# ReGLU MLP: w1 block 0's value half loaded behind four x blocks, the fifth x block turned as 32 bit, two casts moved to VectorE, gate products of three x blocks by one

## The chip, the cores and the metric

The kernel runs on one core of a Trainium2 chip. The metric is the device time in microseconds (us). Before the change it was 309.19 us (median of three runs, 309.01 to 309.37).

Engines are named as in the profile: PE (TensorE matmul), PEld (its weight loads), DVE (VectorE), ACT (ScalarE), POOL (GpSimd), SP (SyncE, which issues the transfers here).

## The reference

```python
# x: 16 x 256 x 512, w1: 512 x 4096, w2: 2048 x 512, all float32
h = x @ w1
gate, value = np.split(h, 2, axis=-1)
h = np.maximum(gate, 0) * value
return (h @ w2).astype(np.float32)
```

## The kernel before

The kernel works on 16 bit operands and saves products by a scheme in which seven products of halves replace eight (P1 to P7 of a block). The scheme needs sums of quarters of x (S1 to S4) and differences of quarters of w1 (T1 to T4). At the start these do not exist yet. So the first two blocks of 128 hidden columns (blocks 0 and 1) are computed plainly, from x as it arrives; from block 2 on the scheme takes over.

The change touches only this opening, about the first 20 us. There x comes as eight blocks of 128 rows by 512 columns, 256 KB each. I count them one to eight: one to four are the first half, `xn[0]` in the code, and five to eight the second. They are transposed on PE ("turned") and copied out of PSUM to 16 bit. A w1 block comes as a gate half and a value half; each is 256 KB for blocks 0 and 1, and 512 KB for the pair 2/3.

```python
fetch_first(0, (0, 1))                       # x blocks one, two
first_w = [load_w1(nc.sync, *wl[0])]         # w1 block 0: gate half, value half
fetch_first(0, (2, 3))
first_w.append(load_w1(nc.sync, *wl[1]))     # w1 block 1: gate half, value half
...
fetch_first(1, range(4))                     # x blocks five to eight
fetch(2, nc.sync); fetch(3, nc.sync)         # w1 blocks 2/3, then 4/5 (one line each in the kernel)
...
plain_w(0, 0, (pool, dve))                   # casts of block 0's gate half
arm(YS[0]); arm(YS[1])
plain[0].open()
plain[0].part("gate", *first_half, cols(0, 2))
plain_w(0, 1, (pool, dve))
keep_busy(4)                                 # filler: products nobody reads
plain[0].part("value", *first_half, cols(0, 2))
turn_first(xo, 0, 2, ...); keep_busy(1); turn_first(xo, 0, 3, ...)
...
plain[1].part("gate", *first_half)           # "block 1's gate": the first use of w1 block 1
cast_first(0, dve); cast_first(1, pool); cast_first(2, pool); cast_first(3, pool)
...
```

At the end of the opening three things come together on DVE and POOL:

```python
for n in ("S1", "S2", "S3"):
    sum_of(sums[1], n)                       # DVE: last sums of x
sum_of(xo, "S4")                             # DVE: two 128 x 1024 inputs in SBUF
held()                                       # DVE: block 1's gate product; frees a PSUM bank
prepare(2, False)
sum_w1(6)                                    # POOL: T1, T2, ... of w1 blocks 2/3
```

Of the kernel before, what the change touches and what calls it, by code (L numbers as in the profile page):

```python
# [16 lines left out]
P = 128  # L17
# [9 lines left out]
@with_exitstack  # L27
def kernel(ctx: ExitStack, tc: tile.TileContext, x, w1, w2, out):






    nc = tc.nc
    x2 = x.flatten_outer_dims()
    out2 = out.flatten_outer_dims()
    flagpool = ctx.enter_context(tc.tile_pool(name="flagpool", bufs=1))
    flag = flagpool.tile([1, 1], dt.int32, name="flag")
    with ExitStack() as fast:  # L40
        unfit = fast_way(fast, tc, x2, w1, w2, out2, flag)
    with tc.If(unfit > 0, label="general"):
        with ExitStack() as general:
            general_way(general, tc, x2, w1, w2, out2)
# [52 lines left out]
def fast_way(ctx, tc, x2, w1, w2, out2, flag):  # L97
# [9 lines left out]
    nc = tc.nc  # L107
# [37 lines left out]
    ident = wpool.tile([P, P], F32, name="ident")  # L145
# [5 lines left out]
    def keep_busy(n):  # L151

        for _ in range(n):
            nc.tensor.matmul(Y[:, :TH // 2], warm_b[:, :P], warm_b[:, :TH // 2], start=False, stop=True,  # L154
                             skip_group_check=True)


    def x_tiles():

        o = {n: xpool.tile([P, 2, TH], F16, name=f"x_{n}", tag=f"x_{n}")  # L160
             for n in ("A11", "A12", "A22", "S1", "S2", "S3", "S4")}
        o["A21"] = o["S3"]
        return o
# [50 lines left out]
    def load_w1(eng, jb, n, u, vs=(0, 1)):  # L214
        t = w_stage[:, u:u + n].rearrange("p u v -> p (u v)").rearrange("p (g e j) -> p g e j", g=2, e=4)
        for v in vs:
            eng.dma_start(out=t[:, v], in_=w1_v[v, :, :, jb * P:(jb + n) * P])
        return t.rearrange("p g (k b) j -> p k b g j", k=2)
# [215 lines left out]
    wl = [(0, 1, 0), (1, 1, 1)] + [(jb, 2, jb % 6) for jb in range(2, NJ, 2)]  # L434
    ws, copies = {}, []

    def fetch(i, eng):
        if i < len(wl):
            assert all(j > i - 3 for j, _ in copies)
            jb, n, u = wl[i]  # L440
            ws[i] = load_w1(eng, jb, n, u)
# [3 lines left out]
    def sum_w1(n=None):  # L445
        for job in w_sums[:n]:
            job()
        del w_sums[:n]

    def prepare(i, at_once=True):  # L450
        jb, n, _ = wl[i]
        copies.extend((i, c) for c in w1_ops(jb, n, ws.pop(i), 1 if i == 2 else n))
        if at_once:
            sum_w1()

    def copy_some(n):
        for _, c in copies[:n]:
            c()
        del copies[:n]

    def plain_w(i, v, engines):

        (jb, n, _), t = wl[i], first_w[i]
        js = slice(jb * P, (jb + n) * P)
        for k, (n, copy) in enumerate(zip((("B11", "B21"), ("T3", "B22"))[v], engines)):
            copy(out=wop[n][:, :, js], in_=t[:, k, :, v])  # L466
# [13 lines left out]
    xn = [[t.rearrange("p a b -> p (a b)").bitcast(F32) for t in place[4 * h:4 * h + 4]] for h in range(2)]  # L480

    x16_first = [halfs.tile([P, 8, P], F16, name="xh", tag="xh").rearrange("p (b q) c -> p b (q c)", b=2) for _ in range(2)]
    ident16 = wpool.tile([P, P], F16, name="ident16")
    half, other = (0, TH // 2), (TH // 2, TH)

    def fetch_first(h, bs):
        for b in bs:
            nc.sync.dma_start(out=xn[h][b], in_=x_nat[0, h, b])  # L488

    def cast_first(b, copy):  # L490
        copy(out=x16_first[b // 2][:, b % 2], in_=xn[1][b])

    def turn_first(o, h, b, places, copies):

        rows, one = (x16_first[b // 2][:, b % 2], ident16) if h else (xn[0][b], ident)
        for k in range(2):
            for e in range(2):
                nc.tensor.transpose(places[k][:, e * P:(e + 1) * P],  # L498
                                    rows[:, (2 * k + e) * P:(2 * k + e + 1) * P], one)
        for k in range(2):  # L500
            copies[k](out=o[f"A{h + 1}{k + 1}"][:, :, b * P:(b + 1) * P],
                      in_=places[k].rearrange("p (b t) -> p b t", b=2))

    def new_x():
        return psx.tile([P, TH], F32, name="X", tag="X")
# [4 lines left out]
    def new_y():  # L510
        return psy.tile([P, TH], F32, name="Y", tag="Y")

    def arm(ps):

        nc.tensor.matmul(ps, warm_b[:, :P], warm_b[:, :TH], start=True, stop=True)

    dve, act, pool = nc.vector.tensor_copy, nc.scalar.copy, nc.gpsimd.tensor_copy
    fetch_first(0, (0, 1))
    first_w = [load_w1(nc.sync, *wl[0])]
    fetch_first(0, (2, 3))  # L520
    first_w.append(load_w1(nc.sync, *wl[1]))
    make_identity(nc, ident)
    fetch_first(1, range(4))
# [3 lines left out]
    xo = x_tiles()  # L527
    plain = [Plain(g, jb) for jb in range(NPLAIN)]
    first_half, second_half = (xo["A11"], xo["A12"]), (xo["A21"], xo["A22"])
    YS = [new_y(), new_y()]  # L530

    def halves(*ts, c=0):
        return [t[:, c:c + 2 * P] for t in ts]

    def turns(t):
        return [t.bitcast(F16)[:, c:c + 2 * P] for c in (0, 2 * P)]

    def cols(b, n=1):
        return b * P, (b + n) * P

    turn_first(xo, 0, 0, halves(*YS), (dve, act))
    XS = [new_x(), new_x()]
    turn_first(xo, 0, 1, halves(*XS), (dve, act))
    plain_w(0, 0, (pool, dve))
    arm(YS[0])
    arm(YS[1])
    plain[0].open()
    plain[0].part("gate", *first_half, cols(0, 2))
    plain_w(0, 1, (pool, dve))
    keep_busy(4)  # L550
    plain[0].part("value", *first_half, cols(0, 2))
    turn_first(xo, 0, 2, halves(*XS, c=2 * P), (dve, act))
    keep_busy(1)
    turn_first(xo, 0, 3, halves(*YS, c=2 * P), (dve, act))
    plain_w(1, 0, (pool, dve))
    plain_w(1, 1, (pool, dve))
    for b in (2, 3):
        for which in ("gate", "value"):
            plain[0].part(which, *first_half, cols(b), False)
    fetch(4, nc.sync)  # L560
    plain[0].value()
    plain[1].open()
    plain[1].part("gate", *first_half)
    cast_first(0, dve)
    cast_first(1, pool)
    cast_first(2, pool)
    cast_first(3, pool)
    plain[1].part("value", *first_half, half)
    turn_first(xo, 1, 0, (turns(YS[0])[0], turns(YS[1])[0]), (dve, act))
    plain[0].gate(0)  # L570
    plain[1].part("value", *first_half, other, False)
    spare = plain[0].X, plain[1].W
    plain[1].value()
# [3 lines left out]
        plain[0].part(which, *second_half, cols(0))  # L577
    turn_first(xo, 1, 1, (turns(YS[0])[1], turns(YS[1])[1]), (dve, act))
    turn_first(xo, 1, 2, (turns(spare[0])[0], turns(spare[1])[0]), (dve, act))
    xo["S3"] = tmp.tile([P, 1024], F16, name="sq", tag="sq", bufs=1).rearrange("p (a b) -> p a b", a=2)  # L580
    sums = [{n: t[:, :, slice(*c)] for n, t in xo.items()} for c in (half, other)]
    sum_of(sums[0], "S1")
# [4 lines left out]
        sum_of(sums[0], n)  # L587
    for which in ("gate", "value"):
        plain[0].part(which, *second_half, cols(2), False)
    for which in ("gate", "value"):  # L590
        plain[0].part(which, *second_half, cols(3), False)
    plain[1].open(*reversed(YS))
    plain[1].part("gate", *second_half)
    for n in ("S1", "S2", "S3"):
        sum_of(sums[1], n)
    sum_of(xo, "S4")
    held()
    prepare(2, False)
    sum_w1(6)
    copy_some(1)  # L600
    plain[0].value()
    plain[0].gate(1)
    copy_some(1)
    prepare(3, False)
    w_sums[:4] = [w_sums[i] for i in (2, 0, 3, 1)]
    sum_w1()
# [49 lines left out]
    rows = []  # L656
# [9 lines left out]
    for s in range(NS):  # L666
# [74 lines left out]
        if s + 1 < NS:  # L741
            xo = xo_next
# [47 lines left out]
```

## Time and profile before

| | before |
|---|---|
| time, median of 3 | 309.19 us |
| PE busy, of the span | 300.7 of 307.5 us |
| 16 DMA engines | full from about 5 to 20 us (0.7 busy from 4 to 5) |
| block 1's gate starts | 10.37 us |
| P1 / P5 / P6 of block 2 start | 16.21 / 17.94 / 18.56 us |
| last product of the kernel starts | 302.66 us |

The profile page's first part gives the busy time of each engine and its share of the span, and its fourth part the chain of waits that ended last.

```profile
PE 300.7 (98%) x1905; PEld 184.0 (60%) x1905; DVE 235.9 (77%) x388; ACT 176.4 (57%) x348; POOL 151.4 (49%) x189
...
PE 96%; DMA 1%; SPq 0%; POOL 0%; ACT 0%; issue 0%
```

PE is the whole chain. So only what makes PE wait in the opening can be worth anything. This is the timeline of PE in the kernel before. Its columns are start, duration, engine, line of the program, operation with output and inputs, shape and count, and in brackets how long the engine had been idle and what ended that.

```profile
6.96 0.61 PE L325 MATMUL X<-x_A,w_B 128*128 128x256 f16 x4 [0.98 <-POOL w_B L466]
7.40 0.60 PE L154 MATMUL Y<-warm 128*128 128x256 f16 x4
...
8.71 0.27 PE L154 MATMUL Y<-warm 128*128 128x256 f16 x1
...
10.37 1.04 PE L325 MATMUL X<-x_A,w_B 128*128 128x512 f16 x4
...
14.17 0.28 PE L498 MATMUL X<-ident,xh 128*128 128x128 f16 x2
...
16.21 0.59 PE L250 MATMUL X<-x_A,w_B 128*128 128x512 f16 x2
...
17.94 0.59 PE L250 MATMUL W<-x_S,w_T 128*128 128x512 f16 x2
18.56 0.60 PE L250 MATMUL Y<-x_S,w_T 128*128 128x512 f16 x2
19.00 0.59 PE L250 MATMUL X<-x_A,w_B 128*128 128x512 f16 x2
...
20.30 0.59 PE L250 MATMUL Y<-sq,w_T 128*128 128x512 f16 x2
```

6.96 is the first gate product; 7.40 and 8.71 are the filler, five products in all. 10.37 is block 1's gate, 14.17 the turn of x block eight, and 16.21, 17.94 and 18.56 are P1, P5 and P6 of block 2. Two products of 128x512 take 0.43 us. So the step from 17.94 to 18.56 (0.62) holds a wait of 0.19, though no bracket shows it: a small gap hides in the modelled ends of the products. Starts are the thing to read here. The 19.00 is P1 of block 3, and 20.30 is P7 of block 2.

Next, the timelines of DVE and of POOL where the two meet, in the kernel before.

```profile
16.15 0.42 DVE L169 TENSOR_TENSOR sq<-x_A,x_S 128x512 f16<-128x512 f16 x1
16.49 0.68 DVE L169 TENSOR_TENSOR x_S<-x_A,x_S 128x1024 f16<-128x1024 f16 x1
17.09 1.28 DVE L334 SCALAR_TENSOR_TENSOR g<-X,v 128x512 f16<-128x512 f32 x2
```

```profile
16.48 1.27 POOL L232 TENSOR_TENSOR w_T<-w_stage 128x256 f16<-128x256 f32 x1 [2.49 <-DMA w_stage<-in_w_dram]
17.83 0.67 POOL L232 TENSOR_TENSOR w_T<-w_stage,w_T 128x256 f16<-128x256 f32 x1
18.46 1.41 POOL L232 TENSOR_TENSOR w_T<-w_stage 128x256 f16<-128x256 f32 x2
```

POOL's first difference (T1) starts 0.14 after its data has landed (16.34) and takes 1.27 us. The same work later takes 0.70 each (the line with x2). It stands behind DVE's sum S4, which started at the same moment. T2 ends at 18.50, and P6, which needs it, starts at 18.56.

**Landings.** Each transfer signals 16 times in the trace; I call the last of the 16 its landing. In this trace: x blocks one and two 3.62 and 4.25, w1 block 0 gate and value 6.32 and 7.11, x three and four 8.13 and 8.82, w1 block 1 gate and value 9.73 and 10.61, x five to eight 11.29, 11.97, 12.65 and 13.33, w1 blocks 2/3 gate and value 14.83 and 16.34. In the timelines a landing shows as the start of the cast that waited for it, 0.02 to 0.06 later.

### The profile page before, as it was taken

What the parts mean: (1) busy time and instruction counts of PE and PEld (TensorE: products, weight loads), DVE (VectorE), ACT (ScalarE), POOL (GpSimd) and SP (SyncE); (2) the same over time, 40 slices, a digit from 0 to 9 for tenths busy, and PEclk for the clock granted to TensorE, in tenths of its full rate; (3) what the DMA queues carried; (4) which work ended last, traced back from release to release, by engine and by line L of the source; (5) the groups of instructions that cost most, each with busy time, mean ns of one, the idle gap of its engine ahead of it and who ended that gap; (6) DMA issues with size and microseconds to landing.
All of it is one profiled execution on the core that took longest, in us unless ns stands there. A gap on an engine that the chain in (4) does not pass through costs nothing.

```text
span 307.5 us, 5285 instructions
## 1 busy us (share of the span) xinstructions
PE 300.7 (98%) x1905; PEld 184.0 (60%) x1905; DVE 235.9 (77%) x388; ACT 176.4 (57%) x348; POOL 151.4 (49%) x189
## 2 busy tenths in 40 slices
PE   7999999999999999999999999999999999999994
PEld 6844444588844444478864444458884444448883
DVE  2579888899768888887438888889536888888841
ACT  2488886455865555538845555546865555553231
POOL 2389999800069899200029889700007998700000
PEclk9999999999999999999999999999999999999998
DMA  6976779964765260001354910000335110001132
GB/s 207 357 257 190 227 177 174 225 123 87 270 193 86 69 136 3 0 0 67 136 175 103 207 34 2 0 2 24 115 108 167 35 34 0 3 1 34 53 120 74
DMA packets 35837, 32.88 MB, mean 107 GB/s; under 512 B 14432, under 2 KB 31328, under 8 KB 35680
## 3 DMA queue, kind: packets, MB, share of 16 engines
q1 hardware_dynamic: 33536, 26.22, 28.0%
q0 software_dynamic: 2272, 6.29, 11.4%
q8 instruction: 16, 0.26, 0.4%
q14 instruction: 13, 0.11, 0.1%
HBM read 27.26 MB, written 12.58 MB: 130 GB/s over the span
## 4 chain that ended last, share of the span: by engine, by line
PE 96%; DMA 1%; SPq 0%; POOL 0%; ACT 0%; issue 0%
PE Y L250 26%; PE X L250 17%; PE W L250 17%; PE Y L362 14%; PE X L362 9%; PE W L362 9%; DMA w_stage<-in_w_dram 1%; PE X L325 1%; PE W L325 1%; PE Y L325 1%; PE Y L498 0%; PE X L498 0%; SPq L488 0%; PE Y L154 0%; POOL w_B L466 0%; ACT o L405 0%
## 5 line engine op out<-in xcount | busy, mean ns | idle before, releaser
L250 PEld LDWEIGHTS <-w_T 128*128 128x128 f16 x496 | 48.3, 98 | 57.3 <-POOL w_T L232 1.1
L179 POOL TENSOR_TENSOR fold<-xh 128x1024 f32<-128x1024 f16 x16 | 30.3, 1894 | 94.5 <-DMA xh<-x 93.7
L250 PE MATMUL X<-x_A,w_B 128*128 128x512 f16 x248 | 73.8, 379 | 0.0
L250 PE MATMUL Y<-x_S,w_T 128*128 128x512 f16 x220 | 65.5, 379 | 0.0
L250 PEld LDWEIGHTS <-w_B 128*128 128x128 f16 x372 | 36.4, 98 | 42.0
L277 DVE SCALAR_TENSOR_TENSOR cc<-W,pu 128x512 f32<-128x512 f32 x62 | 42.9, 691 | 21.2 <-ACT pu L271 20.4
L257 ACT COPY Y<-X 128x512 f32<-128x512 f32 x62 | 35.4, 571 | 38.2 <-PE X L250 37.9
L271 ACT ACTIVATE pu<-Y 128x512 f32<-128x512 f32 x62 | 37.1, 598 | 33.9 <-PE Y L250 32.9
L182 POOL TENSOR_TENSOR fold<-fold 128x512 f32<-128x512 f32 (+2 forms) x96 | 51.8, 539 | 7.5
L362 PEld LDWEIGHTS <-w_stage 128*128 128x128 f16 x512 | 50.0, 98 | 5.8
L287 DVE SCALAR_TENSOR_TENSOR cc<-Y,pu 128x512 f32<-128x512 f32 x62 | 42.9, 691 | 6.7
L282 DVE SCALAR_TENSOR_TENSOR g<-X,cc 128x512 f16<-128x512 f32 x62 | 42.8, 691 | 2.3
L299 DVE SCALAR_TENSOR_TENSOR g<-Y,cc 128x512 f16<-128x512 f32 x62 | 42.2, 681 | 1.8 <-PE Y L250 1.8
L362 PEld LDWEIGHTS <-g 128*128 128x128 f16 x384 | 37.6, 98 | 8.2
L264 ACT ACTIVATE pu<-W 128x512 f32<-128x512 f32 x62 | 37.2, 600 | 0.8 <-PE W L250 0.6
L250 PE MATMUL W<-x_S,w_B 128*128 128x512 f16 x124 | 36.9, 379 | 0.0
L250 PE MATMUL W<-x_S,w_T 128*128 128x512 f16 x124 | 36.9, 379 | 0.0
L250 PE MATMUL Y<-x_A,w_T 128*128 128x512 f16 x124 | 36.9, 379 | 0.0
L362 PE MATMUL X<-w,g 128*128 128x256 f16 x256 | 31.9, 273 | 0.0
L394 DVE SCALAR_TENSOR_TENSOR o<-W,pu 128x256 f32<-128x256 f32 x16 | 6.8, 422 | 19.8 <-PE W L362 19.8
L169 DVE TENSOR_TENSOR w_stage<-g 128x1024 f16<-128x1024 f16 x32 | 21.4, 683 | 0.2
L232 POOL TENSOR_TENSOR w_T<-w_stage 128x512 f16<-128x512 f32 (+1 forms) x16 | 18.7, 1177 | 2.5 <-DMA w_stage<-in_w_dram 2.5
(100 smaller groups left out, 306.2 us busy)
## 6 DMA issues: line engine op xcount, KB each, us to landing
w_stage<-in_w_dram SPq DMA_DIRECT2D x14, 512.0 KB, 6.2
out_dram<-o SPq DMA_DIRECT2D x26, 256.0 KB, 2.1
x<-in_x_dram POOLq DMA_DIRECT2D x4, 1024.0 KB, 9.0
xh<-x SPq DMA_DIRECT2D x16, 256.0 KB, 3.0
w<-in_w_dram POOLq DMA_DIRECT2D x2, 1024.0 KB, 10.2
out_dram<-o SPq DMA_DIRECT2D x12, 128.0 KB, 1.7
w_stage<-in_w_dram SPq DMA_DIRECT2D x4, 256.0 KB, 5.4
x_S<-in_x_dram SPq DMA_DIRECT2D x4, 256.0 KB, 6.1
```

The lines of the kernel that those rows point to most:

```text
L169: eng.tensor_tensor(o[n], o[i0], o[i1], op=op)
L179: nc.gpsimd.tensor_tensor(fold, t, t, op=MULT)
L182: nc.gpsimd.tensor_tensor(fold[:, :, :m], fold[:, :, :m], fold[:, :, m:2 * m], op=ADD)
L250: nc.tensor.matmul(ps, wop[wn][:, b, self.jb * P:(self.jb + 1) * P], self.xo[xn][:, b, :], start=fresh and b == 0, stop=b == 1, skip_group ...
L257: nc.scalar.copy(out=self.Y, in_=self.X)
L264: nc.scalar.activation(self.p5, self.W, COPY, scale=GS)
L271: nc.scalar.activation(self.u2, self.Y, COPY, scale=GS)
L277: nc.vector.scalar_tensor_tensor(out=self.c12, in0=self.W, scalar=GS, in1=self.u2, op0=MULT, op1=ADD)
L282: nc.vector.scalar_tensor_tensor(out=self.g[:, self.jb, :TH], in0=self.X, scalar=0.0, in1=self.c12, op0=MAX, op1=MULT)
L287: nc.vector.scalar_tensor_tensor(out=self.c22, in0=self.Y, scalar=GS, in1=self.p5, op0=MULT, op1=ADD)
L299: nc.vector.scalar_tensor_tensor(out=self.g[:, self.jb, TH:], in0=self.Y, scalar=0.0, in1=self.c22, op0=MAX, op1=MULT)
L362: nc.tensor.matmul(ps, self.op[an][:, i], vop[wn][:, i], start=name in ("P1", "P5") and i == 0, stop=i == NJ // 2 - 1, skip_group_check=True)
```

## The change

The intent is to give PE real work where it ran filler, to start products earlier, and to relieve POOL of two casts.

```diff
     fetch_first(0, (0, 1))
-    first_w = [load_w1(nc.sync, *wl[0])]
+    first_w = [load_w1(nc.sync, *wl[0], (0,))]
     fetch_first(0, (2, 3))
+    load_w1(nc.sync, *wl[0], (1,))
     first_w.append(load_w1(nc.sync, *wl[1]))
@@ opening
+    keep_busy(3)
     plain[0].open()
     plain[0].part("gate", *first_half, cols(0, 2))
+    turn_first(xo, 0, 2, halves(*XS, c=2 * P), (dve, act))
+    turn_first(xo, 0, 3, halves(*YS, c=2 * P), (dve, act))
     plain_w(0, 1, (pool, dve))
-    keep_busy(4)
-    plain[0].part("value", *first_half, cols(0, 2))
-    (turns of x blocks three and four, keep_busy(1) between, column-wise gate and value products)
+    keep_busy(2)
+    plain[0].part("gate", *first_half, cols(2), False)
+    plain[0].part("gate", *first_half, cols(3), False)
+    plain[0].part("value", *first_half)
@@ second half of x
     plain[1].part("gate", *first_half)
-    cast_first(0, dve)
+    plain[0].gate(0)
     cast_first(1, pool)
-    cast_first(2, pool)
-    cast_first(3, pool)
     plain[1].part("value", *first_half, half)
-    turn_first(xo, 1, 0, (turns(YS[0])[0], turns(YS[1])[0]), (dve, act))
-    plain[0].gate(0)
+    turn_first(xo, 1, 0, halves(*YS), (dve, act))        # as 32 bit, no cast
+    cast_first(2, dve)
@@ ...
     turn_first(xo, 1, 2, ...)
+    cast_first(3, dve)
@@ gate products of block 1, three x blocks by one
+    plain[1].open(*reversed(YS))
+    plain[1].part("gate", *second_half, cols(0, 3))
     (last x block of block 0)
-    plain[1].open(*reversed(YS))
-    plain[1].part("gate", *second_half)
+    plain[1].part("gate", *second_half, cols(3), False)
@@ (cut: two ScalarE casts now ahead of plain[0].value())
```

More of the change, by code (lines that the diff above doesn't have):

```diff
@@ L493, in turn_first @@
     def turn_first(o, h, b, places, copies):
-        rows, one = (x16_first[b // 2][:, b % 2], ident16) if h else (xn[0][b], ident)
+        rows, one = (x16_first[b // 2][:, b % 2], ident16) if (h, b) > (1, 0) else (xn[h][b], ident)
         for k in range(2):
@@ L546, in fast_way @@
     arm(YS[1])
+    keep_busy(3)
     plain[0].open()
     plain[0].part("gate", *first_half, cols(0, 2))
+    turn_first(xo, 0, 2, halves(*XS, c=2 * P), (dve, act))
+    turn_first(xo, 0, 3, halves(*YS, c=2 * P), (dve, act))
     plain_w(0, 1, (pool, dve))
-    keep_busy(4)
-    plain[0].part("value", *first_half, cols(0, 2))
-    turn_first(xo, 0, 2, halves(*XS, c=2 * P), (dve, act))
-    keep_busy(1)
-    turn_first(xo, 0, 3, halves(*YS, c=2 * P), (dve, act))
+    keep_busy(2)
+    plain[0].part("gate", *first_half, cols(2), False)
+    plain[0].part("gate", *first_half, cols(3), False)
+    plain[0].part("value", *first_half)
     plain_w(1, 0, (pool, dve))
     plain_w(1, 1, (pool, dve))
-    for b in (2, 3):
-        for which in ("gate", "value"):
-            plain[0].part(which, *first_half, cols(b), False)
     fetch(4, nc.sync)
@@ L599, in fast_way @@
     sum_w1(6)
-    copy_some(1)
+    copy_some(2)
     plain[0].value()
     plain[0].gate(1)
-    copy_some(1)
     prepare(3, False)
```

## The prediction

> **What bounds the kernel now.** The page gives PE 300.7 of 307.5 us busy, and the chain of waits is 96% PE. From 18.6 us on the timeline of PE shows products back to back (two 128x512 every 0.43 us); the change leaves all of that as it is. So only the opening, up to the first sixth product (P6) of block 2 at 18.56 us, can move. There the 16 DMA engines are full from about 4.5 to 19 us (the DMA view), landing 256 KB in 0.7 to 0.9 us. Landings read from the trace: w1 block 0 gate half 6.32 and value half 7.11, x blocks three and four 8.13 and 8.82, w1 block 1 halves 9.73 and 10.61, x blocks five to eight 11.29, 11.97, 12.65, 13.33, w1 blocks 2/3 gate half 14.83, value half 16.34. PE starts block 1's gate at 10.37 because a 0.52 us POOL cast follows the landing at 9.73. P6 waits for POOL's second difference (17.83 to 18.50), and POOL waits for the landing at 16.34. These anchors lie behind the same bytes before and after.
>
> **What the change does.**
> - x blocks three and four land one transfer earlier (about 7.2 and 7.9), the value half about 8.8. PE turns x in place of 0.44 us of filler and computes block 0's value at full width at about 9.4 (landing plus cast), ending about 10.3: just in time for the gate of block 1, which still starts near 10.37. Gain there: nothing; the filler becomes short idle.
> - x block five turned as 32 bit: four transposes 0.43 us, against 0.22 as 16 bit, and its VectorE copy 0.42, against 0.29. The cast (0.43) before it goes. Products of x block five start about 12.59, 0.12 later than now.
> - Casts of x blocks seven and eight go from POOL (0.65, 0.61) to VectorE (0.43 each). The seventh no longer makes PE wait (0.17 now). The eighth stands behind two copies on VectorE, ends about 14.35 instead of 13.99, and its turn starts about 14.4 instead of 14.17.
> - Three-block gate products fill PE while the last copies run; the amount of work is the same.
> - P1 of block 2 then starts about 16.4 (now 16.21), and PE is ready for P6 about 18.55, as now.
> - VectorE's chain of sums ends with S4, now 16.49 to 17.17; I put it 0.25 later, about 17.4. POOL's first difference starts at 16.48 and takes 1.27 instead of 0.7 us, ending 0.58 after S4. The Trainium skill (SBUF — State Buffer, "Who interferes with whom") says that a VectorE operation with two SBUF inputs holds a read port that POOL needs; this trace agrees. So P6 slips to about 18.8. POOL is then continuously busy to 24 us, where PE waits for it again (0.05), so the slip stays.
>
> **Prediction.** About +0.2 us: 309.4 us, range 308.8 to 309.9. Within 2%: 98.5%; faster 1%, slower 0.5%.
>
> **What would show each step.** Gate of block 1 still at 10.3 to 10.5; first products of x block five near 12.6; turn of the eighth near 14.4; POOL's first difference starting near 16.5 and ending near 18.0; P6 near 18.8; every later product shifted by that same amount.
>
> **What would make it wrong.** If POOL gets the port between two sums, its first difference ends near 17.2 and P6 waits only for PE: no change, or a little faster. If VectorE's sums come earlier than I think, P6 could start up to 0.6 us earlier. If the value half lands after 9.0, the rest shifts later by the excess. A different skew of the 16 queues would move all landings. A PE clock drop in the new gaps before 9.4 would cost more; the page shows full clock there now.

## The result, and the profile after

| | before | after |
|---|---|---|
| time, median of 6 runs each | 309.35 us (309.01 to 309.65) | 309.43 us (308.88 to 309.75) |
| ratio | | 1.000, 95% interval 0.9987 to 1.0013 |
| PE busy, of the span | 300.7 of 307.5 us | 301.1 of 308.0 us |
| block 1's gate starts | 10.37 | 10.61 |
| P1 / P5 / P6 of block 2 start | 16.21 / 17.94 / 18.56 | 16.54 / 18.26 / 18.69 |
| last product starts | 302.66 | 302.89 |

A ratio is the mean time of one kernel's fast runs over that of the other's of the same rounds, so it is not quite the ratio of the medians.

The lines that answer to those of before, first from the page:

```profile
PE 301.1 (98%) x1901; PEld 184.5 (60%) x1901; DVE 237.0 (77%) x389; ACT 176.2 (57%) x348; POOL 150.1 (49%) x187
...
PE 95%; DMA 2%; SPq 1%; POOL 0%; issue 0%; ACT 0%; DVE 0%
```

The timeline of PE after:

```profile
6.21 0.49 PE L154 MATMUL Y<-warm 128*128 128x256 f16 x3
7.33 0.61 PE L325 MATMUL X<-x_A,w_B 128*128 128x256 f16 x4 [0.64 <-POOL w_B L466]
...
8.72 0.38 PE L154 MATMUL Y<-warm 128*128 128x256 f16 x2
8.94 0.68 PE L325 MATMUL X<-x_A,w_B 128*128 128x128 f16 x8
9.71 0.60 PE L325 MATMUL W<-x_A,w_T 128*128 128x512 f16 x2
10.15 0.59 PE L325 MATMUL W<-x_A,w_B 128*128 128x512 f16 x2
10.61 1.04 PE L325 MATMUL X<-x_A,w_B 128*128 128x512 f16 x4
...
14.54 0.28 PE L498 MATMUL X<-ident,xh 128*128 128x128 f16 x2
...
16.54 0.59 PE L250 MATMUL X<-x_A,w_B 128*128 128x512 f16 x2
...
18.26 0.59 PE L250 MATMUL W<-x_S,w_T 128*128 128x512 f16 x2
18.69 0.59 PE L250 MATMUL Y<-x_S,w_T 128*128 128x512 f16 x2
19.12 0.59 PE L250 MATMUL X<-x_A,w_B 128*128 128x512 f16 x2
...
20.52 0.59 PE L250 MATMUL Y<-sq,w_T 128*128 128x512 f16 x2
```

6.21 and 8.72 are the moved filler. The rest of block 0's gate products start at 8.94 and need 0.44, then PE stands until the value half has landed and is cast (9.71): 0.33 us, as much as the three filler products that ran behind the first gate product before (0.11 each). P6 now follows P5 by 0.43, without a wait. A new small one is at 20.52 (P7 of block 2): four steps of 0.43 or 0.44 from 18.69 end at 20.42, so PE waited 0.10 there. The timeline of ACT after shows for what: P7 writes the bank that ACT reads for P6 (line 271), and that read, queued behind those of P5 (line 264) and of block 1 (line 330), ended at 20.46.

```profile
18.89 0.60 ACT L264 ACTIVATE pu<-W 128x512 f32<-128x512 f32 x1 [0.62 <-PE W L250]
19.39 0.59 ACT L330 ACTIVATE v<-Y 128x512 f32<-128x512 f32 x1
19.86 0.60 ACT L271 ACTIVATE pu<-Y 128x512 f32<-128x512 f32 x1
```

So P7 now hangs on P5 by way of ACT, and an earlier P6 gains little: P7 starts 2.25 or 2.26 after P5 in after and in eight later traces, against 2.36 in the three traces whose P6 waited (in the two that are left, k4 and d2, a product ahead of P7 waited).

DVE and POOL after:

```profile
16.53 0.42 DVE L169 TENSOR_TENSOR sq<-x_A,x_S 128x512 f16<-128x512 f16 x1
16.86 1.22 DVE L169 TENSOR_TENSOR x_S<-x_A,x_S 128x1024 f16<-128x1024 f16 x1
18.00 1.28 DVE L334 SCALAR_TENSOR_TENSOR g<-X,v 128x512 f16<-128x512 f32 x2
```

```profile
16.60 0.93 POOL L232 TENSOR_TENSOR w_T<-w_stage 128x256 f16<-128x256 f32 x1 [3.87 <-DMA w_stage<-in_w_dram]
17.61 1.00 POOL L232 TENSOR_TENSOR w_T<-w_stage,w_T 128x256 f16<-128x256 f32 x1
18.57 1.41 POOL L232 TENSOR_TENSOR w_T<-w_stage 128x256 f16<-128x256 f32 x2
```

The order at the port is turned round. POOL's T1 now gets in ahead of S4, and S4 takes 1.22 instead of 0.68. No engine shows this as idle: the loser's instruction is recorded as a longer one.

From 31 us to the end the two traces are the same stream of products, 0.23 apart all the way (checked every 50 products). So everything that the change did to PE is in the opening, and it is +0.23 us in this pair of traces. But block 1's gate was already 0.24 late, and so was the landing before it: 9.98 after against 9.73 before. Whether this is the change or chance, one pair of traces cannot tell.

### The profile page after: what moved, and what is told of

It is laid out like the page before. It is cut to its first block, busy times and chain, and to the rows that moved or that the text cites. A ratio compares the mean times of both kernels' runs of the same rounds, so it can differ in the third digit from the quotient of the medians.

```text
span 308.0 us, 5277 instructions
## 1 busy us (share of the span) xinstructions
PE 301.1 (98%) x1901; PEld 184.5 (60%) x1901; DVE 237.0 (77%) x389; ACT 176.2 (57%) x348; POOL 150.1 (49%) x187
## 4 chain that ended last, share of the span: by engine, by line
PE 95%; DMA 2%; SPq 1%; POOL 0%; issue 0%; ACT 0%; DVE 0%
PE Y L250 26%; PE X L250 17%; PE W L250 17%; PE Y L362 14%; PE W L362 9%; PE X L362 9%; DMA w_stage<-in_w_dram 2%; PE W L325 1%; PE X L325 1%; SPq L488 1%; PE Y L325 1%; PE Y L498 0%; POOL w_T L466 0%; SPq L217 0%; ACT o L405 0%
```

## The experiments

**Theory.** The landings set the pace. PE can do its work in the opening in any order; it always ends up waiting for w1 block 1's gate half and what lands behind it, so the filler that was moved away turns into waiting. The second half of the change trades small costs for small gains. **Rival 1:** the filler was on the critical path, moving three of its products ahead of the first gate product is a real gain, and the second half gives it back. **Rival 2** (my prediction): POOL's differences hold P6 and set the end.

All transfers come in the same order behind w1 block 1's gate half. So for each trace I measure from its landing to the start of the kernel's last product. This takes the chance of the landings out. All kernels in one table (starts in us after that landing; the landing itself in the second column):

| run | landing | block 1's gate | P1 of block 2 | P5 of block 2 | last product |
|---|---|---|---|---|---|
| before, first trace | 9.73 | 0.64 | 6.48 | 8.21 | 292.93 |
| before, again (r1) | 9.19 | 0.74 | 6.47 | 8.20 | 292.92 |
| opening only (a1) | 9.91 | 0.64 | 6.47 | 8.20 | 292.93 |
| after, first trace | 9.98 | 0.63 | 6.56 | 8.28 | 292.91 |
| after, again (r2) | 9.50 | 0.64 | 6.58 | 8.30 | 292.93 |
| rest only (b1) | 9.98 | 0.70 | 6.62 | 8.34 | 292.96 |
| cast on ACT (k3) | 9.88 | 0.60 | 6.56 | 8.29 | 292.91 |
| casts on POOL (c1) | 9.79 | 0.66 | 6.52 | 8.25 | 292.88 |
| one more load (e1) | 9.84 | 0.63 | 6.55 | 8.28 | 292.91 |
| split value half (k4) | 9.56 | 0.64 | 6.56 | 8.28 | 293.36 |
| split, held first (h1) | 10.17 | 0.64 | 6.56 | 8.29 | 292.91 |
| combined (g1) | 9.93 | 0.66 | 6.63 | 8.36 | 292.99 |
| before, less x (d1) | 8.93 | 1.40 | 7.10 | 8.82 | 293.45 |
| after, less x (d2) | 8.57 | 1.31 | 7.22 | 8.95 | 293.95 |

In the ten traces with the last product at 292.88 to 292.96 the landing lies anywhere from 9.19 to 10.17. Measured from the first gate product instead, the same ten spread from 295.28 to 296.43, so it is not a chain from that product that binds. The table can't single out one landing: from that of x block eight, for one, the ten spread by 0.15, little more than the 0.08 here.

Times follow with each run. Their medians scatter by some tenths, more than most effects here, so verdicts rest on the table. It has one trace of each kernel but two of before and of after.

### r1 and r2: both kernels traced again

No edit.

> The kernel before, unchanged, traced a second time: how far do landings and PE times move without any change? In the first trace of before, block 1's gate started at 10.37, the first P1 of block 2 at 16.21 and the last product at 302.66 us; in the trace of after 10.61, 16.54 and 302.89. If the difference of 0.24 at block 1's gate is noise of the transfers, this trace will scatter by 0.1 to 0.3 and may come near 10.6. If it comes from the new order of the transfers, it will repeat 10.37 within 0.05.

> The changed kernel, unchanged, traced a second time. Noise theory: block 1's gate may start anywhere from 10.3 to 10.7, last product 302.6 to 303.0. Order theory: 10.6 again, last product 302.9. My prediction's theory (P6 held up by POOL, 18.8): the first trace did not show it, P6 started 0.43 after P5 without a wait; if it shows here, P6 starts more than 0.5 after P5.

Measured: the landing of w1 block 1's gate half was 9.19 in the second trace of before and 9.50 in that of after, against 9.73 and 9.98 in the first ones. It scatters by half a microsecond with no change at all. The last product came at 302.11 and 302.43, and moved with the landing: 292.92 and 292.93 after it. The "order" theory expected 10.37 and 10.61 again and is out. The +0.23 of the first pair is the +0.25 of its landings. The signals show where the scatter arises: the first of the 16 signals of this transfer came at 8.12 and 7.93 (before) and at 8.14 and 8.16 (after), and the last of them 1.61, 1.27, 1.84 and 1.34 later. P6 followed P5 by 0.43 in r2, so my prediction's slip did not show here either.

In r1 the gate started 0.74 after the landing, 0.10 later than in the first trace, and P1 did not move. So between gate and P1 there is slack, and what is waited for there lands later still (x blocks five to eight).

### a1: the opening alone

```diff
 (before, with:)
+ w1 block 0's value half loaded behind x blocks three and four
+ keep_busy(3), turns of x three and four, keep_busy(2), gate columns, value at full width
- keep_busy(4), keep_busy(1), column-wise products
```

> Only the first half of the change: order of the transfers, x blocks three and four turned in place of filler, block 0's value at full width. All that follows as before. If the transfers set the pace of the opening, block 1's gate starts at the landing of its weights plus 0.62 (0.52 of cast), as in before and after, whatever order PE had, and the time is 309.4 plus or minus 0.3. If the filler taken out (0.44 to 0.55 us) had been on the critical path, the last product comes 0.3 to 0.5 earlier than in before.

Measured: 310.35 us (308.28 to 311.43, four runs), before 308.96 in the same rounds, ratio 1.003 (0.9983 to 1.0076). The gate started 0.64 after the landing and the last product 292.93 after it, as in before. Taking three filler products out of the stretch from the first gate product to block 1's gate gained nothing on PE, which rules out rival 1. The time's median is 1.4 above that of before and outside my band. In the one trace most of this is in the tail: the last transfer of the output landed 4.16 us after the last product, with one of its 16 signals 1.57 behind all others (3.15 and 3.26 in the two traces of before). Whether the other runs had the same is open.

### b1: the rest alone

```diff
 (before's opening, with:)
+ x block five as 32 bit, casts of x seven and eight on DVE, plain[0].gate(0) earlier, gate cols(0, 3) then cols(3)
```

> Only the second half of the change: x block five turned as 32 bit, two casts on VectorE, gate products of three x blocks by one. The opening as before. From block 1's gate to the first P1 of block 2 before took 5.84 us and after 5.93. If the cost of after lies here, this run takes 5.9 to 6.0 between the two, although its gate starts near 10.4; time 309.3 to 309.6. If this half is a gain on its own (less waiting for POOL's casts) that a worse opening ate, it takes less than 5.8 and the last product comes near 302.5.

Measured: 309.48 us, before 308.96, ratio 1.0017 (1.0000 to 1.0033). Gate to P1 took 5.92, as expected under "the cost lies here" (before 5.84 and 5.73). P5 came 0.13 later after the landing than in before, but the last product only 0.03 later. So this half costs PE about 0.1 up to P5, and almost all of it is given back before the end: P6 no longer waits for POOL, because T1 now goes ahead of S4, and only part of that is lost again at P7.

### d1 and d2: one x block less to load (wrong result)

```diff
-    fetch_first(0, (2, 3))
+    fetch_first(0, (2,))          # x block four's rows are read from block three's
```

> Wrong result on purpose: the kernel before, but x block four is not loaded (its rows are those of block three), so every later transfer lands about 0.69 earlier. In six traces so far the last product came 292.91 to 292.96 us after the landing of w1 block 1's gate half, whatever the kernel, so the landing sets the pace. Landing theory: with less to wait for, PE's own order binds; from first gate product to block 1's gate before took 3.41 and needs about 3.2 (work 2.6, filler 0.55), so the last product comes 0.2 earlier relative to the first gate product and the distance from the landing grows to 293.3 to 293.5. Rival (some chain of engines binds, the landing is incidental): distance grows by the whole 0.69 and the time does not change.

> Wrong result on purpose: the changed kernel with the same load left out. Landing theory: without the filler PE's own order from first gate product to block 1's gate needs about 2.85 against 3.2 of before, so here the change should show what it is worth: the changed kernel ends 0.2 to 0.35 us earlier than the kernel before with the same load left out, measured from the first gate product. Rival: both the same.

Measured, d1: 309.47 us, before 309.16, ratio 1.0002 (0.9976 to 1.0029); d2: 309.30, ratio 1.0005 (0.9987 to 1.0023). With one load less, PE's own order binds: from first gate product to block 1's gate d1 took 3.26 (7.07 to 10.33) and d2 2.91 (6.97 to 9.88), close to the 3.2 and 2.85 expected. The distance from the landing to the last product grew to 293.45 in d1, inside the 293.3 to 293.5 of the landing theory; the rival's 293.6 is not far off, and the times do not separate the two. The 0.35 between d1 and d2 is not a gain of the new opening. It is the three filler products that now stand ahead of the first gate product, where a count from that product leaves them out. In d2 they ran right up to it (6.65 to 6.97), although the last operand was ready at 6.55 (ACT's copy of x block two), so they held it up by about what was saved behind it. And from the first gate product to the last product d1 took 295.31 and d2 295.55: the changed kernel was 0.24 slower, where I had expected it 0.2 to 0.35 faster. The trace of d2 shows where: P1 of block 3 waited.

```profile
6.65 0.49 PE L154 MATMUL Y<-warm 128*128 128x256 f16 x3
6.97 0.60 PE L325 MATMUL X<-x_A,w_B 128*128 128x256 f16 x4
...
17.95 0.59 PE L250 MATMUL Y<-x_S,w_T 128*128 128x512 f16 x2
18.93 0.59 PE L250 MATMUL X<-x_A,w_B 128*128 128x512 f16 x2 [0.38 <-DVE g L334]
```

The last two lines are P6 and P1 of block 3, a step of 0.98 instead of 0.43. DVE's product g (line 334) frees the PSUM bank, and it stood behind S4, which stood behind POOL.

### k3: one cast on ACT

```diff
-    plain_w(1, 0, (pool, dve))
+    plain_w(1, 0, (act, dve))
```

> The changed kernel with one cast of w1 block 1's gate half on ScalarE (0.37) in place of POOL (0.52). If the chain is landing, cast, PE to the end, block 1's gate starts 0.47 after the landing (now 0.63) and the last product 292.78 after it (now 292.92). If what binds is the later landing of w1 blocks 2/3 with POOL's differences (my prediction), the last product stays at 292.92 and PE waits at P6 of block 2. Time 309.2 to 309.3, within noise either way.

Measured: 309.29 us, before 309.16, ratio 1.0003 (0.9981 to 1.0025). The gate started 0.60 after the landing, not 0.47, and the last product came 292.91 after it. The expectation missed: in the changed kernel the cast of w1 block 1 is not what the gate waits for. Block 0's value products end only at that moment (9.61 plus 0.87 is 10.48), because they themselves wait for the value half that the change moved back. In the first trace of after the two landings meet there within 0.03 us: the value products end at 10.58 (9.71 plus 0.87), and the gate starts at 10.61. P6 did not wait for POOL, so rival 2 was not confirmed either.

### k4: the value half of w1 blocks 2/3 in two transfers

```diff
         for v in vs:
+            if jb == 2 and v:
+                for j in range(n):
+                    eng.dma_start(out=t[:, v, :, j * P:(j + 1) * P],
+                                  in_=w1_v[v, :, :, (jb + j) * P:(jb + j + 1) * P])
+                continue
```

> The changed kernel with the value half of w1 blocks 2/3 loaded as two transfers, block 2 first, so POOL's first difference can start about 0.7 earlier (near 15.8). If POOL's differences bind (my prediction), the last product comes 0.1 to 0.3 earlier, near 292.7 after the landing of w1 block 1's gate half. If PE's chain from that landing binds, it stays at 292.92.

Measured: 310.04 us, before 309.16, ratio 1.0030 (1.0011 to 1.0048); the last product 293.36 after the landing, later than either theory expected (0.44 later than 292.92). T1 did start earlier, at 15.72, and T2 ended at 17.26. POOL was then ahead at the port, and DVE's last sums came late. The timelines of POOL, DVE and PE in k4:

```profile
15.72 0.72 POOL L237 TENSOR_TENSOR w_T<-w_stage 128x256 f16<-128x256 f32 x1 [3.27 <-DMA w_stage<-in_w_dram]
16.53 0.73 POOL L237 TENSOR_TENSOR w_T<-w_stage,w_T 128x256 f16<-128x256 f32 x1
```

```profile
16.65 0.89 DVE L169 TENSOR_TENSOR sq<-x_A,x_S 128x512 f16<-128x512 f16 x1
17.46 1.21 DVE L169 TENSOR_TENSOR x_S<-x_A,x_S 128x1024 f16<-128x1024 f16 x1
18.60 1.28 DVE L339 SCALAR_TENSOR_TENSOR g<-X,v 128x512 f16<-128x512 f32 x2
```

```profile
18.27 0.59 PE L255 MATMUL Y<-x_S,w_T 128*128 128x512 f16 x2
19.33 0.59 PE L255 MATMUL X<-x_A,w_B 128*128 128x512 f16 x2 [0.46 <-DVE g L339]
```

A 128x512 sum that takes 0.42 alone took 0.89, S4 1.21 instead of 0.68, and P1 of block 3 waited for the product behind them. So relieving POOL of its wait moved the wait to DVE.

### h1: k4 with the product ahead of the sum

```diff
-    sum_of(xo, "S4")
-    held()
+    held()
+    sum_of(xo, "S4")
```

> The kernel with the split value half (which lost 0.43 by the last product, 293.36) with one more change: VectorE computes block 1's first gate product (which frees the PSUM bank that P1 of block 3 waits for) before the sum S4 and not after it. If the loss came from S4 standing behind POOL at the port and holding up that product, P1 of block 3 no longer waits (0.46 now) and the last product comes at 292.9. If the loss has another cause, it stays at 293.3.

Measured: the last product 292.91 after the landing, as expected; P1 of block 3 follows P6 by 0.43. This shows the cause of k4's loss. The trace of d2 has the same wait behind the same product; there the cause is likely the same, but it was not tested. The timeline of DVE in h1:

```profile
18.10 0.68 DVE L339 SCALAR_TENSOR_TENSOR g<-X,v 128x512 f16<-128x512 f32 x1
18.70 0.68 DVE L169 TENSOR_TENSOR x_S<-x_A,x_S 128x1024 f16<-128x1024 f16 x1
19.30 0.68 DVE L339 SCALAR_TENSOR_TENSOR g<-X,v 128x512 f16<-128x512 f32 x1
```

The time was 310.16 us, before 309.07, ratio 1.0027 (1.0008 to 1.0046), although PE lost nothing. Part of that has a place: from the last landing to the end of the span k4, h1, g1 and e1, which have one transfer more, took 2.19 us. The ten other traces took 1.65 to 1.71. The records of SyncE in the packed trace show why (the timeline leaves them out). At the end it waits for eight DMA semaphores, which the transfers use in turn, one after another in a fixed order, about 0.08 us each. With 110 transfers the last one to land is on the eighth of them, and one wait follows. With 111 it is on the first, and all eight follow: 0.62 from the landing to the end of these waits, against 0.08. With 109 (d1, d2) two follow, 0.15.

### c1: the two casts on POOL again

```diff
     cast_first(1, pool)
+    cast_first(2, pool)
+    cast_first(3, pool)
-    cast_first(2, dve)
-    cast_first(3, dve)
```

> The changed kernel with the casts of x blocks seven and eight on POOL again. VectorE has 0.86 us less to do, so its last sum S4 starts about 0.4 earlier and should be ahead of POOL's first difference at the port again: S4 0.7 (now 1.22), first difference 1.25 (now 0.8 to 0.93). PE then waits for POOL at P6 as in before. From block 1's gate to P1 of block 2: 5.85 (now 5.93). Last product 292.9 after the landing of w1 block 1's gate half, so nothing gained or lost. Rival: if the casts on VectorE are what costs 0.1, the last product comes 0.1 earlier, 292.8.

Measured: 309.60 us, before 309.07, ratio 1.0013 (0.9995 to 1.0031). The expectation about the port failed: S4 started 0.23 after the landing of T1's data, against 0.41 in the first trace of after, so 0.18 earlier and not 0.4, and POOL was still ahead (T1 0.76, S4 1.22). PE did not wait at P6. Gate to P1 took 5.86. The last product came 292.88 after the landing: moving the casts is worth 0.03 to 0.05 us in this one trace.

### e1: one load more

```diff
     fetch_first(0, (2, 3))
+    nc.sync.dma_start(out=(unused part of the w2 buffer), in_=x_nat[1, 0, 0])   # nobody reads it
     load_w1(nc.sync, *wl[0], (1,))
```

> The changed kernel with one more x block (256 KB that nobody reads) loaded just ahead of w1 block 0's value half, so that half and all later transfers land about 0.69 later. In three traces with this order of transfers the last product came 294.71 to 294.72 us after the landing of x block four and 292.91 to 292.93 after that of w1 block 1's gate half. If the transfers set the pace: 295.4 after x block four, still 292.9 after w1 block 1's gate half, and a time 0.7 above that of before in the same rounds. If PE or another engine sets it: 294.7 to 295.0 after x block four and less than 292.6 after w1 block 1's gate half, time within 0.3.

Measured: 310.51 us, before 309.07, ratio 1.0048 (1.0029 to 1.0067), so about 1.5 us slower. The last product came 292.91 after w1 block 1's gate half landed, as the landing theory said. But this trace tests it weakly, because the half did not land later than without the extra load (9.84, against 9.50 to 10.17 in the other traces of this order). Its first signal did come 0.64 later than in the first trace of after (8.78 against 8.14), but its last came 1.06 behind the first and not 1.84. The other anchor failed: it came 296.18 after the landing of x block four, not 295.4, because in this trace the gate half landed 3.27 after x four (1.80 in the first trace of after), so x four's landing is a poor anchor. Of the 1.5 us, 0.54 lies in the end of the program (2.19 against 1.65). The 0.7 that was expected of the landings is not in this trace, which is one of the faster runs (309.91); whether it is in the others is not known.

### g1: combined

```diff
 (h1, with:)
-    turn_first(xo, 1, 0, halves(*YS), (dve, act))                 # 32 bit
+    cast_first(0, dve)                                            # ahead of plain[0].gate(0)
+    turn_first(xo, 1, 0, (turns(YS[0])[0], turns(YS[1])[0]), (dve, act))
-    cast_first(2, dve)
+    cast_first(2, pool)
```

> The kernel of the run before in this list, with x block five cast to 16 bit on VectorE and turned as 16 bit (0.22 of PE less, smaller copies), its gate product after that cast, and x block seven cast on POOL. PE's chain from block 1's gate to P1 of block 2 should be 5.7 (now 5.92) and no engine should then hold PE by more than 0.1, so the last product comes near 292.7 after the landing of w1 block 1's gate half, 0.2 us less than both kernels: the best version that these findings allow, though less than the scatter of the times. Rival: some other wait takes it back, 292.9.

Measured: 310.08 us, before 309.07, ratio 1.0024 (1.0006 to 1.0042). Gate to P1 took 5.97, not 5.7, and the last product came at 292.99. The rival expectation was nearer. The 0.22 us of PE that the 16 bit turn saves went into waiting for the x blocks: x block eight was turned at 14.56, because its cast on DVE (14.09) stood behind two copies there, as in the changed kernel. No version found here beats both kernels.

## Why the prediction was right or wrong

The time was right: 309.4 predicted, 309.43 measured, range 308.8 to 309.9. Point by point:

- *"These anchors lie behind the same bytes before and after"*: right, and stronger than I had put it. In ten traces, of eight kernels and two repeats, all with no bytes taken away and no wait for a bank, the last product came 292.88 to 292.96 us after one landing (g1 292.99).
- *"Gain there: nothing; the filler becomes short idle"*: right. PE stood 0.33 before 9.71, and a1 gained nothing. But the prediction speaks of the filler as replaced, and three of its five products were only moved ahead. Block 0's value started at 9.71 and not 9.4, as the landings of that trace were later (9.08 against my 8.8).
- *32 bit turn, 0.12 later; turn of x block eight near 14.4*: the first products of x block five began at 12.82, 2.84 after the landing, against 2.74 in before, so 0.10 later. The turn of x eight came at 14.54, 4.56 after the landing, against 4.44, so 0.12 later; I had said 0.23.
- *P1 about 16.4*: 16.54 in a trace whose landing was 0.25 late; after the landing it is 0.08 later than before (6.56 against 6.48), where I had said 0.19.
- *"So P6 slips to about 18.8 ... so the slip stays"*: this step failed, though 18.69 and +0.23 look like it. POOL did not stand behind S4. It took the port first, T1 lasted 0.93 instead of the 1.5 that I had counted (16.5 to 18.0), and P6 followed P5 without a wait. This was my first named alternative, "POOL gets the port between two sums". The +0.23 of the traces came from the landing (+0.25), which r1 and r2 show to be chance, so that it agrees with my +0.2 is luck. The change's own effect, -0.02 to +0.01 us by the table, is what opposite terms leave. In after's first trace P5 comes 0.08 later after the landing. Gone are the waits of 0.19 at P6 and 0.05 near 24 us; new are waits of 0.10 at P7, for ACT, and 0.06 right behind it. The sum is zero. The prediction does not name ACT, whose queue takes back most of what POOL's earlier difference gives.
- *A PE clock drop in the new gaps*: the granted clock did not drop (0.997 against 0.996).

So the prediction's total was right for the most part because its largest term, the landings, was right. Its +0.2 was a term that did not exist, and it is below the scatter of the times, which cannot tell +0.2 from zero.

What stays open: why the landing of the same transfer scatters from 9.19 to 10.17 between runs with the same bytes ahead of it (in these eleven traces its last signal lags the first by 1.27 to 1.86; the prediction had named such a skew as a risk); and a1's slow tail. Also untested is the version that g1 points to, with x block eight cast away from DVE's queue.

## What to carry to other kernels

Before moving work inside an opening, find the landing that everything waits for and measure each trace from it; here that brought the repeats of one kernel from 0.5 us apart to 0.02. Filler that PE ran while a transfer was on its way cost nothing here, and taking it out of that stretch gained nothing. Look where it goes, too: set ahead of the first product, it held that product up in the run whose data was there early (d2). If DVE and POOL share a port, releasing one of them earlier hands its wait to the other: look at what stands behind the loser, and put the instruction that frees a bank ahead of the one that has to fight for the port.

## What the Trainium skill lacked or had wrong

- "SBUF — State Buffer", section "Who interferes with whom", says that a DVE instruction with two SBUF inputs contends with a POOL instruction that reads SBUF. It adds that the port is held exclusively and that issue order decides who blocks. These traces agree in both directions: S4 first, T1 took 1.27 (0.70 alone); T1 first, S4 took 1.22 (0.68 alone). What the section does not say is how this looks in a profile: the loser shows no idle time and no wait, only a longer duration.
- The same section lacks how small a shift turns this order round: S4 started 0.15 us after the landing of T1's data in before and won, and 0.23 after it in c1 and lost.
- "TensorE: Matmul & The Clock Gate", section "What's actually happening", says that the warm-up takes about 3.4 us in a free-running window, so that its end varies from run to run, by 500 ns either way. These traces agree that it varies, but by more: the first product starts at 1.27 or 1.28 in all fourteen, and the slow pace (two turns every 0.43 us instead of every 0.22) ends at about 4.7 in the first trace of before and at about 6.8 in r2. The four turns of x block two took 0.60 in the first trace of before and 1.06 in r1, although the profile's table of windows shows a granted clock of 1.00 over the first 20 us of r1. Together with the moved filler it made the first gate product of r2 wait for PE, not for data, and cost nothing at the end.
- "DMA: Bandwidth & Descriptors", section "Why a DMA increments its semaphore by 16 and not by 1", says that the engines of one transfer finish independently and only the full 16 means landed. It lacks the size: in the first trace of before the first signal of w1 block 0's gate half came at 4.75 and the last at 6.32, and 1.6 us between first and last (1.9 for x block three) stayed for all transfers up to w1 blocks 2/3. For w1 block 1's gate half it was 1.06 to 1.86 in the fourteen traces.
- No page that I read has the 0.54 us that one more transfer added between the last landing and the end of the program (2.19 against 1.65): seven more of SyncE's waits for DMA semaphores, 0.08 us each.
